# Next group's first tile turned among the last value products, mixers paced with their loads a step later, and the seventh head outputs turned beside the sixth's product

## The chip, the cores and the metric

The kernel runs on one core of a Trainium2 chip. The metric is device time in microseconds (us) from the first to the last instruction of the program with what lies around it; the median of the runs counts. TensorE (PE in the profile) does the matrix products and the transposes; VectorE (DVE), ScalarE (ACT) and GpSimd (POOL) move results out of the product banks (PSUM) and do the elementwise work; SyncE (SP) issues most of the transfers.

## The reference, cut to what matters

One step of a one-layer streaming encoder on 1024 prompt tokens and 32 sample tokens, model width 1024, everything in 32-bit floats:

```python
h = mixer(rms_norm(x, g_mix_pre))        # three parallel head groups, then cat @ w_out
x = x + rms_norm(h, g_mix_post)
h = conv_ffn(rms_norm(x, g_ffn_pre))     # up, causal conv, gelu(gate) * val, down
x = x + rms_norm(h, g_ffn_post)

# mixer
proj = xn @ w_in                          # queries, keys, values, decays and gates of all heads
o_a, s_gla  = gated_linear_scan(...)      # 6 heads, chunks of 64 tokens, masked scores + carried state
o_b, s_hg   = gated_linear_scan(...)      # 5 heads
h,  (c,n,m) = mlstm_scan(...)             # 5 heads, after a causal conv over q and k
cat = concat(head_rms_norm(o_a)*silu(.), head_rms_norm(o_b)*silu(.), head_rms_norm(h)*sigmoid(.))
return cat @ w_out
```

The states of the scans and the last rows of both convolutions are outputs too.

## The kernel before, in words

Each product of two 32-bit matrices is made of three products of rounded parts (high times high, low times high, high times low), written by one helper, `mm3`, so that lines 88, 89 and 90 of the profile are most of TensorE's work.

The program goes through the tokens in this order. **Input products:** three groups of 384, 384 and 256+32 tokens. For each group `inproj(g)` makes 14 feature products (`pf`, queries, keys, decays, with features on the partitions) and 8 blocks of value and gate products (`pv`, with tokens on the partitions; `pv1_7` is unit 1 of block 7, a unit u being 128 tokens). The group's normalised tokens are first turned by TensorE (`xt`, two banks of four 128x128 transposes a unit), then split into a high part `xh` by ScalarE and a low part `xl` by VectorE; `norm_group` is the generator that does one unit a step. **Mixers:** beside the products of the next group, `mixer(u)` runs the scans of one unit in 12 steps: the scores `sc` in steps of growing decay range (`sc0_0`, `sc0_2`, `sc0_4` for unit 0, all in one bank, each copied out by VectorE with a mask into `P` before the next may write), small transposes `mi`, the outputs `og`, `oh`, `om`, `oi` (two banks that take turns), and the normalised, gated result `cat`, which goes to memory (`cat_d`). **Output product:** for u in the order 0, 1, 2, 3, 8, 4, 5, then 6 and 7, `outproj(u)` loads `cat` again (`ct`), turns it in two halves (`ctp`), splits it (`ch`, `cl`), multiplies (`zp`, 24 products of 512 columns for each half), normalises, adds the residual, normalises again and turns the result for the FFN (`fxt`). `pipeline` interleaves the seven units of `RING`, beside the last mixers. **FFN:** up and down products by a scheme with sums of blocks ahead of and behind fewer products (`pux`, `puw`, `us`, `q`, `x` and others); at the very end four tiles `q30` to `q33` are added, squared, scaled and stored.

Generators set the rough order. `merge(main, nmain, nside)` advances the mixers' generator in step with the main one's, evenly. Within that a scheduler with a modelled timeline sets the order on each engine, moved by priorities (`high_priority`), by `issue_after` and by which bank or buffer is free: product results share three banks (`big`), scores have one (`sc`), head outputs two (`o`). Each engine goes through its own list in that order, and so do the queues that issue transfers.

Of the kernel before, what the change touches and what calls it, by code (L numbers as in the profile page):

```python
# [8 lines left out]
F32 = mybir.dt.float32  # L9
# [69 lines left out]
def body(ctx: ExitStack, tc: tile.TileContext, a: dict):  # L79
# [128 lines left out]


# [144 lines left out]
    def inproj(g, xh, xl, normed, scaled=None):  # L354
# [77 lines left out]
        def vg(blk):  # L432
            ws = vg_weights(blk)
            N = 256 if blk else 282
            for i, (u, off, n) in enumerate(units_of(g)):
# [10 lines left out]
                vg_store(blk, u, off, n, ps)  # L446
                yield
# [283 lines left out]
    def mixer(u, g, ci0):  # L731
# [17 lines left out]
        v = mx.tile([128, 704], F32, tag="v", name=f"v{u}", bufs=1)  # L749
        sp.dma_start(v[:n], v_d[t0:t0 + n, :704])  # L750
        vmt = vm[0]
        sp.dma_start(vmt[:n, :, :64], v_d[t0:t0 + n, 704:].rearrange("t (h d) -> t h d", d=64))
        gt = mx.tile([128, 1024], F32, tag="gt", name=f"gt{u}", bufs=1)
        sp.dma_start(gt[:n], g_d[t0:t0 + n, :])
# [22 lines left out]
        yield  # L777

# [24 lines left out]
        yield  # L803

# [229 lines left out]
        if u == 7:  # L1034
            ct_of[u] = cat
        else:
            sp.dma_start(cat_d[t0:t0 + n, :], cat[:n])
# [28 lines left out]
    def outproj(p2, W, u):  # L1066
# [9 lines left out]
        for hf in range(2):  # L1076
# [36 lines left out]
        def leave(ps, hf):  # L1113

            act.activation(z[:n, cs[hf]], ps[:n], AF.Square, accum_out=ss[:n, hf:hf + 1])
# [33 lines left out]
        else:  # L1149
# [11 lines left out]
        pool.tensor_tensor(ss[:n, 2:3], ss[:n, 0:1], ss[:n, 1:2], op=ALU.add)  # L1161
        rstd_of(ss[:n, 3:4], ss[:n, 2:3], n, 1, 1024)
# [27 lines left out]
        for hf in range(2):  # L1190
            p, t, b = (upper[0], "xw", 4) if u == 5 else (upper[0], *(("xw", 4), ("sx", 1))[hf]) if 5 < u < 8 else (psb, "big", 3)
# [19 lines left out]
    def pipeline(gens):  # L1211
# [5 lines left out]
        for i, x in enumerate(gens):  # L1217
            after = gens[i + 1:i + 2]
# [446 lines left out]
    def down_all(ph, pc, begun, late):  # L1665
# [43 lines left out]
        def square_of(u, n, src, half, ss):  # L1709
            jk = pc.tile([128, 512], BF16, tag="fjk", name=f"gjk{u}{half}", bufs=2)  # L1710
            act.activation(jk[:n], src, AF.Square, accum_out=ss[:n, 2 + half:3 + half])  # L1711
# [5 lines left out]
        def scale_of(n, ss):  # L1717
            pool.tensor_tensor(ss[:n, 0:1], ss[:n, 2:3], ss[:n, 3:4], op=ALU.add)  # L1718
            rstd_of(ss[:n, 1:2], ss[:n, 0:1], n, 1, 1024)
# [148 lines left out]
        for i in range(4):  # L1868
# [4 lines left out]
            dve.tensor_tensor(CA[:, i, 1], CA[:, i, 1], W[i], op=ALU.add)  # L1873
# [311 lines left out]
```

## Time and profile before

| | |
|---|---|
| runs | 1342.25, 1338.36, 1338.61 us; median 1338.61 |
| profiled execution | 1338.15 us, its span 1336.4 us |
| mean clock granted to TensorE | 0.990 |
| TensorE busy | 1295.7 us, 97% of the span |
| VectorE, ScalarE, GpSimd busy | 1009.2, 700.0, 284.6 us |

The span runs from the first to the last instruction; the 1.75 us beside it lie around it. TensorE is busy nearly always, and the view of its waits covers the rest; in some stretches its clock is granted at half (`PEclk` in the views by stretch: 1.00 is full). A wait view lists, for each line of an engine, what ended its idle time, and how often.

### The profile page before, as it was taken

To read this page: it belongs to the slowest core of one execution; us is meant where nothing else is said; L and a number is where in the kernel's file an instruction comes from. 1 tells how busy PE (TensorE), PEld (TensorE's weight loads), DVE (VectorE), ACT (ScalarE), POOL (GpSimd) and SP (SyncE) were. 2 spreads that over 40 slices of the span, in tenths; PEclk is the share of its full clock that TensorE was granted. 3 is DMA by queue.
4 is the path that set the end of the run, shared out by engine and by line. 5 is a ranking of instruction groups with operands and counts; after the bars stand their busy time and mean duration, and the time that the engine had idled before them with its cause. 6 is when DMAs were issued, how large, how long until landed. Compare 5 with 4: busy or idle time off the path is not lost.

```text
span 1336.4 us, 25589 instructions
## 1 busy us (share of the span) xinstructions
PE 1295.7 (97%) x9896; PEld 1097.9 (82%) x9896; DVE 1009.2 (76%) x1761; ACT 700.0 (52%) x1298; POOL 284.6 (21%) x400
## 2 busy tenths in 40 slices
PE   6999999998999999999999999999999999999997
PEld 6999899998898987867887777778888887778885
DVE  5795659768588778785898776778888976499556
ACT  5655556554575555444764444444555454454552
POOL 4532302135022163223110010111110000020005
PEclk9999999999998999989999999999999999999999
DMA  9799878886789954534436988864665349844425
GB/s 336 246 360 367 280 258 260 275 278 214 260 263 309 330 180 163 184 111 135 143 133 216 365 223 284 213 185 135 158 162 145 88 147 350 330 146 148 139 87 126
DMA packets 134785, 291.73 MB, mean 218 GB/s; under 512 B 29016, under 2 KB 63992, under 8 KB 132536
## 3 DMA queue, kind: packets, MB, share of 16 engines
q1 hardware_dynamic: 120887, 266.51, 58.4%
q0 software_dynamic: 9264, 19.14, 7.8%
q10 hardware_dynamic: 4512, 4.46, 1.0%
q8 instruction: 77, 1.26, 0.4%
q14 instruction: 45, 0.36, 0.1%
HBM read 229.38 MB, written 85.78 MB: 236 GB/s over the span
## 4 chain that ended last, share of the span: by engine, by line
PE 63%; DVE 9%; ACT 2%; issue 1%; POOL 1%; DMA 0%; DVEq 0%; POOLq 0%; ACTq 0%
PE pux_None L88 4%; PE pux_None L90 4%; PE pux_None L89 4%; PE puw_None L89 3%; PE puw_None L90 3%; PE puw_None L88 3%; PE q L88 3%; PE q L89 3%; PE q L90 3%; PE x L88 2%; PE x L89 2%; PE x L90 2%; PE zp L88 2%; PE zp L90 2%; PE zp L89 2%; PE us L1475 2%
## 5 line engine op out<-in xcount | busy, mean ns | idle before, releaser
L1442 DVE SCALAR_TENSOR_TENSOR y<-uu,fconv_sb,y 128x1024 f32<-128x1024 f32 x88 | 112.8, 1281 | 24.7 <-ACT y L1440 23.7
L1439 POOL COPY fhalo<-uu 128x2 f32<-128x2 f32 x44 | 19.3, 439 | 380.7 <-DVE uu L1352 380.7
L1440 ACT ACTIVATE y<-uu,fconv_sb 128x1024 f32<-128x1024 f32 x44 | 54.7, 1244 | 12.8 <-DVE uu L1352 12.2
L88 PE MATMUL pv<-wt_0h,xh 128*128 128x256 f32 (+1 forms) x192 | 56.0, 292 | 2.8 <-DVE xl L319 1.6
L90 PE MATMUL zp<-woh,cl 128*128 128x512 f32 (+1 forms) x144 | 57.0, 396 | 1.5 <-DVE cl L1091 1.5
L88 PE MATMUL zp<-woh,ch 128*128 128x512 f32 (+1 forms) x144 | 56.5, 401 | 0.7 <-ACT ch L1090 0.7
L89 PE MATMUL zp<-wol,ch 128*128 128x512 f32 (+1 forms) x144 | 56.9, 395 | 0.0
L90 PE MATMUL pv<-wt_1h,xl 128*128 128x256 f32 (+1 forms) x192 | 55.1, 287 | 0.0
L90 PE MATMUL pv<-wt_0h,xl 128*128 128x256 f32 (+1 forms) x192 | 54.8, 286 | 0.0
L88 PE MATMUL pv<-wt_1h,xh 128*128 128x256 f32 (+1 forms) x192 | 54.8, 285 | 0.0
L89 PE MATMUL pv<-wt_0l,xh 128*128 128x256 f32 (+1 forms) x192 | 54.7, 285 | 0.0
L89 PE MATMUL pv<-wt_1l,xh 128*128 128x256 f32 (+1 forms) x192 | 54.5, 284 | 0.0
L206 POOL TENSOR_SCALAR hrs<-hss 128x5 f32<-128x5 f32 (+3 forms) x27 | 10.1, 375 | 174.2 <-DVE hss L1000 170.3
L1718 POOL TENSOR_TENSOR gss<-gss 128x1 f32<-128x1 f32 (+1 forms) x9 | 9.8, 1092 | 174.2 <-ACT gjk L1711 174.2
L816 DVE COPY_PREDICATED P<-masks_sb,sc 128x352 f32<-128x352 int32 (+3 forms) x53 | 37.8, 713 | 6.0 <-PE sc L729 5.4
L88 PEld LDWEIGHTS pv<-wt_0h,xh 128*128 128x128 f32 x192 | 36.2, 188 | 4.3 <-DVE xl L319 1.9
L88 PEld LDWEIGHTS pv<-wt_1h,xh 128*128 128x128 f32 x192 | 36.2, 189 | 0.7 <-issue 0.6
L1000 DVE TENSOR_REDUCE hss<-sq 128x5 f32<-128x320 f32 (+3 forms) x27 | 13.5, 502 | 30.7 <-ACT sq L999 30.6
L207 POOL TENSOR_TENSOR hrs<-hrs,mhalf 128x5 f32<-128x5 f32 (+3 forms) x27 | 36.2, 1341 | 2.2
L90 PEld LDWEIGHTS pv<-wt_0h,xl 128*128 128x128 f32 x192 | 36.4, 189 | 0.2
L89 PEld LDWEIGHTS pv<-wt_0l,xh 128*128 128x128 f32 x192 | 36.3, 189 | 0.1
L89 PEld LDWEIGHTS pv<-wt_1l,xh 128*128 128x128 f32 x192 | 36.2, 189 | 0.1
(1899 smaller groups left out, 4639.9 us busy)
## 6 DMA issues: line engine op xcount, KB each, us to landing
wus<-in_w_us SPq DMA_DIRECT2D x16, 1024.0 KB
wrP<-in_w_dn SPq DMA_DIRECT2D x27, 512.0 KB, 3.7
ht<-h_d SPq DMA_DIRECT2D x22, 512.0 KB, 7.9
wt_0r<-in_w_tok SPq DMA_DIRECT2D x21, 512.0 KB, 6.0
wt_1r<-in_w_tok SPq DMA_DIRECT2D x21, 512.0 KB, 6.1
h_d<-y SPq DMA_DIRECT2D x21, 512.0 KB, 4.4
ws_d<-in_w_dn POOLq DMA_DIRECT2D x20, 512.0 KB, 7.0
wrP<-ws_d SPq DMA_DIRECT2D x20, 512.0 KB, 3.9
```

Source lines behind the costliest of these rows:

```text
L88: pe.matmul(ps, lh[0], rh[0], start=first, stop=False, **kw)
L89: pe.matmul(ps, lh[0], rh[1], start=False, stop=False, **kw)
L90: return pe.matmul(ps, lh[1], rh[0], start=False, stop=last, **kw)
L206: pool.tensor_scalar(out, ss, 1.0 / width, eps, op0=ALU.mult, op1=ALU.add)
L207: pool.tensor_tensor(out, out, mhalf[:n, :cols], op=ALU.pow)
L816: dve.copy_predicated(dst, mk.broadcast_to([n, 11, *mk.shape[2:]]), src)
L1000: dve.tensor_reduce(ss[:n, h0:h0 + nh], sq3, axis=mybir.AxisListType.X, op=ALU.add)
L1439: behind["POOL"] = pool.tensor_copy(fhalo[:, j, :], u[:, SEQ - 2:SEQ])
L1440: act.activation(y, u, AF.Identity, scale=fconv[:, j, 2:3], bias=fconv[:, j, 3:4])
L1442: dve.scalar_tensor_tensor(y, uu[i][:, s:s + SEQ], fconv[:, j, s:s + 1], y, op0=ALU.mult, op1=ALU.add)
L1475: kept["us"] = pe.matmul(ps[DEC * q:DEC * q + DEC], smp_x[:, k, :], ring[i % 3][:, q, :], start=k == 0, stop=k == 7)
L1718: pool.tensor_tensor(ss[:n, 0:1], ss[:n, 2:3], ss[:n, 3:4], op=ALU.add)
```

## The change

It has six parts. (1) The high and low parts of all groups lie in one pair of tiles, of which each group takes a slice, so that a transpose of the next group needs only its own columns free; and the next group's `norm_group` takes its first step right after the first unit of value block 7. (2) A mixer's loads of `v`, and of `vm` and `gt`, are issued one and two steps later, and the store of `cat` goes to GpSimd's queue in place of SyncE's. (3) In the third group the mixers are advanced by a table, `PACE`: pairs of (step of the main generator, mixer steps done by then). (4) In the output product, unit 6 yields after each half, and `pipeline` takes it as the successor of unit 5, so its halves are turned beside unit 5's product; `fxt` of unit 4 goes to the head outputs' banks. (5) The two sums of squares of a row are added by the instruction that also adds epsilon (the squares are scaled in ScalarE), which takes one GpSimd instruction from each such chain. (6) The last additions of `q` get a higher priority.

```diff
+    def rstd_of_halves(out, m0, m1, n):
+        pool.tensor_scalar(out, m0, m1, EPS, op0=ALU.add, op1=ALU.add)
+        pool.tensor_tensor(out, out, mhalf[:n, :1], op=ALU.pow)
@@ norm_tiles, inproj @@
-        return (p1.tile([128, 8, T], F32R, tag="xh", name=f"xh{g}"),
-                p1.tile([128, 8, T], F32R, tag="xl", name=f"xl{g}"))
+        if not normal:
+            normal.extend(p1.tile([128, 8, GROUPS[0][1]], F32R, name=f"x{c}_all") for c in "hl")
+        return [t[:, :, :T] for t in normal]
-    def inproj(g, xh, xl, normed, scaled=None):
+    def inproj(g, xh, xl, normed, following, scaled=None):
                 vg_store(blk, u, off, n, ps)
+                if blk == 7 and not i:
+                    next(following)
                 yield
@@ mixer: the loads of v, vm and gt leave the first step @@
-        v = mx.tile([128, 704], F32, tag="v", name=f"v{u}", bufs=1)
-        sp.dma_start(v[:n], v_d[t0:t0 + n, :704])
-        vmt = vm[0]
-        sp.dma_start(vmt[:n, :, :64], v_d[t0:t0 + n, 704:].rearrange("t (h d) -> t h d", d=64))
-        gt = mx.tile([128, 1024], F32, tag="gt", name=f"gt{u}", bufs=1)
-        sp.dma_start(gt[:n], g_d[t0:t0 + n, :])
...
         yield
+        v = mx.tile([128, 704], F32, tag="v", name=f"v{u}", bufs=1)
+        sp.dma_start(v[:n], v_d[t0:t0 + n, :704])
...
         yield
+        vmt = vm[0]
+        sp.dma_start(vmt[:n, :, :64], v_d[t0:t0 + n, 704:].rearrange("t (h d) -> t h d", d=64))
+        gt = mx.tile([128, 1024], F32, tag="gt", name=f"gt{u}", bufs=1)
+        sp.dma_start(gt[:n], g_d[t0:t0 + n, :])
...
-            sp.dma_start(cat_d[t0:t0 + n, :], cat[:n])
+            pool.dma_start(cat_d[t0:t0 + n, :], cat[:n])
@@ outproj @@
-            if u in RING:
+            if u != 7:
                 yield
-        if u not in RING:
+        if u == 7:
             yield
-            act.activation(z[:n, cs[hf]], ps[:n], AF.Square, accum_out=ss[:n, hf:hf + 1])
+            act.activation(z[:n, cs[hf]], ps[:n], AF.Square, scale=1.0 / 32, accum_out=ss[:n, hf:hf + 1])
-        pool.tensor_tensor(ss[:n, 2:3], ss[:n, 0:1], ss[:n, 1:2], op=ALU.add)
-        rstd_of(ss[:n, 3:4], ss[:n, 2:3], n, 1, 1024)
+        rstd_of_halves(ss[:n, 3:4], ss[:n, 0:1], ss[:n, 1:2], n)
-            p, t, b = (upper[0], "xw", 4) if u == 5 else ...
+            p, t, b = (psm, "o", 2) if u == 4 else (upper[0], "xw", 4) if u == 5 else ...
-    def pipeline(gens):
+    def pipeline(gens, then):
-            after = gens[i + 1:i + 2]
+            after = (gens + [then])[i + 1:i + 2]
@@ end of the FFN @@
-            pool.tensor_tensor(ss[:n, 0:1], ss[:n, 2:3], ss[:n, 3:4], op=ALU.add)
-            rstd_of(ss[:n, 1:2], ss[:n, 0:1], n, 1, 1024)
+            rstd_of_halves(ss[:n, 1:2], ss[:n, 2:3], ss[:n, 3:4], n)
-            dve.tensor_tensor(CA[:, i, 1], CA[:, i, 1], W[i], op=ALU.add)
+            with tc.high_priority(offset=AHEAD):
+                dve.tensor_tensor(CA[:, i, 1], CA[:, i, 1], W[i], op=ALU.add)
@@ merge and the calls @@
-    def merge(main, nmain, nside):
+    def merge(main, nmain, nside, pace=None):
             want = (i + 1) * nside // nmain
+            for (i0, s0), (i1, s1) in zip(pace or (), (pace or ())[1:]):
+                if i0 <= i < i1:
+                    want = s0 + (i + 1 - i0) * (s1 - s0) // (i1 - i0)
+    PACE = ((0, 0), (3, 3), (10, 12), (17, 15), (NIN, 3 * NMIX))
+    normed = [norm_group(g, *norm_tiles(g)) for g in range(3)] + [None]
-        merge(inproj(g, *xs_, norm_group(g, *xs_), scaled), NIN, n_side)
+        merge(inproj(g, *xs_, *normed[g:g + 2], scaled), NIN, n_side, PACE if g == 2 else None)
-    merge(pipeline(firsts), 26, 3 * NMIX + 2)
+    last = [outproj(p2, wo, u) for u in (6, 7)]
+    merge(pipeline(firsts, last[0]), 26, 3 * NMIX + 2)
     pump(1000)
-    last = [outproj(p2, wo, u) for u in (6, 7)]
-    for x in (last[0], last[0], last[1]):
+    for x in last:
         next(x)
```

What the edits do to the order, at three places. First TensorE at the end of group 0, where unit 0's scores and the last value products meet (`pv1_7`, `pv2_7`: units 1 and 2 of block 7; `xt30`: the first half of unit 3's tokens). Before (the rows begin at `pv1_7`'s last three of 24 products):

```order
L88 MATMUL pv1_7_1638<-wt0_7_1h_1602,xh0_162 128x256
L89 MATMUL pv1_7_1638<-wt0_7_1l_1603,xh0_162 128x256
L90 MATMUL pv1_7_1638<-wt0_7_1h_1602,xl0_163 128x256
L729 MATMUL mi_159<-ident_123,kh0_1891 128x128
L729 MATMUL sc0_2_2090<-Qz1_153,k0_1816 64x2x32
L729 MATMUL sc0_2_2090<-Qz1_153,k0_1816 64x32
L729 MATMUL sc0_2_2090<-Qz1_153,k0_1816 64x2x32
L729 MATMUL sc0_2_2090<-Qz1_153,k0_1816 64x32
L729 MATMUL sc0_2_2090<-Qz1_153,k0_1816 64x2x32 x4
L729 MATMUL sc0_2_2090<-Qz1_153,k0_1816 64x32 x2
L88 MATMUL pv2_7_1669<-wt0_7_0h_1595,xh0_162 128x256
```

and now, from the last of `sc0_0` on:

```order
L738 MATMUL sc0_0_1978<-Qz0_152,Ld0_150 32x32 x8
L738 MATMUL mi_159<-ident_123,kh0_1886 128x128
L322 MATMUL xt30_1638<-ident_123,x3_1144 128x128 x4
L738 MATMUL mi_159<-ident_123,kh0_1886 128x128 x3
L738 MATMUL sc0_2_2088<-Qz1_153,k0_1828 64x2x32
L738 MATMUL sc0_2_2088<-Qz1_153,k0_1828 64x32
L738 MATMUL sc0_2_2088<-Qz1_153,k0_1828 64x2x32
L738 MATMUL sc0_2_2088<-Qz1_153,k0_1828 64x32
L738 MATMUL sc0_2_2088<-Qz1_153,k0_1828 64x2x32 x4
L738 MATMUL sc0_2_2088<-Qz1_153,k0_1828 64x32 x4
L322 MATMUL xt31_1645<-ident_123,x3_1144 128x128 x4
...
L88 MATMUL pv1_7_1652<-wt0_7_0h_1595,xh_all_162 128x256
```

`pv1_7` stood between `sc0_0` and `sc0_2` and now stands behind both, with unit 3's transposes in its place.

Next TensorE in the seventh unit's mixer, behind its second group of scores. Before:

```order
L88 MATMUL zp81_8323<-woh7_6898,ch81_8034 32x512
L89 MATMUL zp81_8323<-wol7_6906,ch81_8034 32x512
L90 MATMUL zp81_8323<-woh7_6898,cl81_8035 32x512
L1086 MATMUL ctp41_8386<-ident_123,ct4_7889 128x128 x4
L1195 MATMUL fxt30_8395<-ident_123,z3_7845 128x128 x4
L729 MATMUL sc7_4_8179<-Qz1_153,Ld1_151 64x2x32
L729 MATMUL sc7_4_8179<-Qz1_153,Ld1_151 64x32
```

and now:

```order
L738 MATMUL sm7_8105<-ident_123,mqk7_7899 128x64
L1205 MATMUL fxt30_8387<-ident_123,z3_7838 128x128 x4
L1205 MATMUL fxt31_8393<-ident_123,z3_7838 128x128 x4
L88 MATMUL zp40_8429<-woh0_6887,ch40_8246 128x512
...
L90 MATMUL zp40_8429<-woh7_6894,cl41_8384 128x512
L1097 MATMUL ctp50_8458<-ident_123,ct5_8239 128x128 x4
L738 MATMUL sc7_4_8171<-Qz1_153,Ld1_151 64x2x32
L738 MATMUL sc7_4_8171<-Qz1_153,Ld1_151 64x32
```

The third group of scores, `sc7_4`, followed four transposes; now the 24 products of `zp40` (its first and last stand here) and another tile's transposes lie ahead of it.

Last TensorE between unit 5's output product (`zp51` is its second half) and unit 6's. Before:

```order
L90 MATMUL zp51_8566<-woh7_6898,cl51_8509 128x512
L1195 MATMUL fxt40_8593<-ident_123,z4_8437 128x128 x4
L1195 MATMUL fxt41_8599<-ident_123,z4_8437 128x128 x4
L1086 MATMUL ctp60_8616<-ident_123,ct6_8465 128x128 x4
L1086 MATMUL ctp61_8625<-ident_123,ct6_8465 128x128 x4
L88 MATMUL zp60_8635<-woh0_6891,ch60_8621 128x512
L89 MATMUL zp60_8635<-wol0_6899,ch60_8621 128x512
```

and now:

```order
L90 MATMUL zp50_8529<-woh7_6894,cl51_8500 128x512
L1097 MATMUL ctp60_8556<-ident_123,ct6_8456 128x128 x4
L88 MATMUL zp51_8565<-woh0_6887,ch50_8463 128x512
...
L90 MATMUL zp51_8565<-woh7_6894,cl51_8500 128x512
L1205 MATMUL fxt40_8601<-ident_123,z4_8428 128x128 x4
L1097 MATMUL ctp61_8592<-ident_123,ct6_8456 128x128 x4
L1205 MATMUL fxt41_8607<-ident_123,z4_8428 128x128 x4
L88 MATMUL zp60_8624<-woh0_6887,ch60_8561 128x512
L89 MATMUL zp60_8624<-wol0_6895,ch60_8561 128x512
```

Unit 6's first half (`ctp60`) was turned behind all of `zp51` and is turned ahead of it; the second (`ctp61`) stands between the two `fxt40`, `fxt41`.

More of the change, by code (lines that the diff above doesn't have):

```diff
@@ L272, in norm_tiles @@
         T = GROUPS[g][1] + GROUPS[g][2]
-        return (p1.tile([128, 8, T], F32R, tag="xh", name=f"xh{g}"),
-                p1.tile([128, 8, T], F32R, tag="xl", name=f"xl{g}"))
+        if not normal:
+            normal.extend(p1.tile([128, 8, GROUPS[0][1]], F32R, name=f"x{c}_all") for c in "hl")
+        return [t[:, :, :T] for t in normal]
+    normal = []
     xn_of, vgi, vcopies, gate = {}, [], [], []
@@ L1156, in outproj @@
                 with tc.high_priority(offset=AHEAD):
-                    kept["jk"] = act.activation(jk, pss[hf], AF.Square, accum_out=ss[:, hf:hf + 1])
+                    kept["jk"] = act.activation(jk, pss[hf], AF.Square, scale=1.0 / 32, accum_out=ss[:, hf:hf + 1])
         load_res(u)
@@ L1190, in outproj @@
         for hf in range(2):
-            p, t, b = (upper[0], "xw", 4) if u == 5 else (upper[0], *(("xw", 4), ("sx", 1))[hf]) if 5 < u < 8 else (psb, "big", 3)
+            p, t, b = (psm, "o", 2) if u == 4 else (upper[0], "xw", 4) if u == 5 else (upper[0], *(("xw", 4), ("sx", 1))[hf]) if 5 < u < 8 else (psb, "big", 3)
             ps = p.tile([128, 4, 128], F32, tag=t, name=f"fxt{u}{hf}", bufs=b)
@@ L1710, in square_of @@
             jk = pc.tile([128, 512], BF16, tag="fjk", name=f"gjk{u}{half}", bufs=2)
-            act.activation(jk[:n], src, AF.Square, accum_out=ss[:n, 2 + half:3 + half])
+            act.activation(jk[:n], src, AF.Square, scale=1.0 / 32, accum_out=ss[:n, 2 + half:3 + half])
         def norm_of(u, n, src, half, ss):
```

## Prediction

> **What bounds the kernel.** I read the page first, for the engines' shares and the clock; then TensorE's waits, which say what its idle time is made of; then the timeline around each long one; and last the views by stretch, for the granted clock.
>
> ```profile
> span 1336.4 us, 25589 instructions
> PE 1295.7 (97%) x9896; PEld 1097.9 (82%) x9896; DVE 1009.2 (76%) x1761; ACT 700.0 (52%) x1298; POOL 284.6 (21%) x400
> ...
> PE xt L315 <- DVE x L295: 9.6, 1, 9.6
> PE sc L729 <- DVE P L816: 3.4, 3, 2.4
> PE ctp L1086 <- DMA ct<-cat_d: 1.5, 1, 1.5
> ```
>
> TensorE is the bound: its 1295.7 us leave 40.7 us of the span, of which 9.6 are the start (first wait row) and, by the tail's rows below, 9.6 the end (the last product is done at 1326.76). So 21.5 us of idle time lie between, in many places of at most 2.4, and no other engine is near its limit over the whole. The change can only remove or add such places, and shorten the end. The clock is the second thing to win. It was granted at half in four places ahead of the end; three follow a long wait:
>
> ```profile
> 326.25:329.66 3.41, 1.72 (x67) 1.40 (x68) 3.41 (x9) 3.39 (x8) 1.35 (x2) 1.00 0.72 166
> 329.66:333.07 3.41, 3.41 (x16) 3.40 (x16) 3.41 (x14) 1.70 (x5) 1.93 (x2) 0.50 0.67 268
> 411.60:415.00 3.40, 1.82 (x71) 1.81 (x71) 3.39 (x8) 1.69 (x4) 0.39 (x2) 1.00 1.05 366
> 415.00:421.80 6.80, 6.80 (x62) 6.19 (x62) 5.91 (x13) 1.43 (x4) 0.00 (x0) 0.50 0.75 210
> 493.50:496.90 3.40, 3.24 (x54) 2.56 (x52) 3.21 (x11) 3.40 (x4) 3.03 (x5) 1.00 0.78 192
> 496.90:500.30 3.40, 3.40 (x28) 3.01 (x26) 3.34 (x5) 3.40 (x5) 0.00 (x0) 0.50 1.01 319
> 585.70:589.10 3.40, 0.96 (x20) 0.75 (x22) 3.39 (x9) 1.51 (x4) 1.33 (x4) 1.00 0.67 200
> 589.10:595.90 6.80, 6.80 (x119) 6.13 (x111) 6.36 (x12) 1.15 (x2) 0.44 (x2) 0.50 0.23 76
> ```
>
> The columns behind the stretch are its length, then TensorE's busy time, weight loads, VectorE, ScalarE, GpSimd, and the clock. A stretch of 3.4 us in which TensorE was busy for 1.72, 1.82 or 0.96 us is followed by 3.4 or 6.8 us at 0.50. Ahead of the fourth (493.5) it was busy for 3.24. In 3.4 us at half clock TensorE does at most 1.7 us of work, so each costs at most 1.7, less where what runs in it hangs on other engines. [...]
>
> **The change, place by place.** A gain has a plus.
>
> *Groups 0 to 1: unit 3's transposes ahead of `sc0_2`, `pv1_7` behind it.*
>
> ```profile
> 141.72 0.39 PE L88 MATMUL pv<-wt_0h,xh 128*128 128x256 f32 x1 [0.83 <-DVE vth L425]
> 144.60 0.52 DVE L816 COPY_PREDICATED P<-masks_sb,sc 128x352 f32<-128x352 int32 x1
> 145.22 0.54 PE L729 MATMUL sc<-Qz,k 64*64 64x64 f32 x20 [0.28 <-PE mi L729]
> 145.40 0.68 DVE L836 TENSOR_TENSOR x<-b 128x512 f32<-128x512 f32 x1
> ```
>
> `pv1_7` fills 141.72 to about 144.8, and meanwhile VectorE gets to the masked copy of `sc0_0` (done at 145.12), for which `sc0_2` must wait since scores have one bank. VectorE's order up to that copy is the same afterwards. So `xt30` starts at 141.72 in place of `pv1_7` (the same bank comes free), takes about 0.7 us, the `mi` 0.4, and from about 142.9 TensorE stands until 145.2: 2.3 us that `pv1_7` covered. Then `pv1_7` waits for the split of `xt30`, whose VectorE half comes behind the row at 145.40 and takes 0.68: 146.76, another 0.4 us. The transposes themselves are only moved (1.3 us less later), and a gap of 0.3 us behind them goes. Bounds: 0, if VectorE were free sooner, and -2.9; I take -2.4. The cover is gone here, so the clock counts: of any 3.4 us from 142 on, TensorE would be busy for about 1.0, within the three rows above. One stretch at half clock, of which 2 us hold large products, costs 1.0 to 1.7: I take -1.2. Sum -3.6.
>
> *Groups 1 to 2.*
>
> ```profile
> 322.44 0.81 PE L729 MATMUL oi<-C,mqz 128*64 128x65 f32 x20 [0.90 <-DVE cat L1002]
> 325.43 0.66 PE L315 MATMUL xt<-ident,x 128*128 128x128 f32 x4 [0.72 <-ACT vth L98]
> 329.45 0.45 PE L88 MATMUL pv<-wt_0h,xh 128*128 128x282 f32 x1 [1.64 <-DVE xl L319]
> ```
>
> Unit 6's transposes now stand behind `pv3_7`, covered; but `oi2`, now ahead of `pv5_7`, meets VectorE's `cat` some 0.8 us too early in addition to its 0.90, and `pv5_7` waits about 0.55 for `xl`. Against that the 0.72 goes and the 1.64 shrinks, since one unit's turn is left to do there. The half-clock stretch behind 329.66 may move to 323 or go. Bounds -1.5 and +3; I take +0.8.
>
> *Group 2, paced.*
>
> ```profile
> 368.20 0.75 PE L729 MATMUL oh<-S,qz 128*64 128x64 f32 x20
> 384.28 0.80 PE L729 MATMUL oi<-C,mqz 128*64 128x65 f32 x20 [0.84 <-DVE cat L1002]
> 398.82 0.44 PE L729 MATMUL mi<-ident,kh 128*128 128x128 f32 x2 [0.38 <-ACT kt L877]
> 401.66 0.55 PE L729 MATMUL sc<-Qz,k 64*64 64x64 f32 x24 [0.68 <-DVE P L816]
> 413.18 1.14 PE L729 MATMUL sc<-Qz,Ld 64*64 64x64 f32 x64 [2.15 <-DVE e L543]
> ```
>
> `oi3` needs the bank of `oh3`, and with it VectorE's `cat` of `oh3`, which came only some 15 us behind `oh3` (368.95 to 384.28), since the group's gate rows stand ahead of it on VectorE. `oi3` moves from 95 feature products behind `oh3` to 53, but those gate rows now lie behind `cat`: laid end to end from the durations of before, `cat` is done about 8 us behind `oh3` and `oi3` reached after about 9. So +0.84; if the gate rows come in between after all, 42 products of cover are missing, 5 us by the value products' 0.12 each (24 from 141.72 to about 144.8), and it is -3. `sc4_0` and `sc4_2` find their operands ready (+0.38, +0.68). `sc4_4` still has 48 feature products for cover, about 8.1 us with the small ones; but VectorE no longer has the mLSTM score product (0.68), a decay product (0.42) and some of the convolution (0.5 each) between `sc4_2` and its second masked copy, so that chain, laid end to end, is about 8.7 us, where it was about 10.3: a wait of 0.6 remains of 2.15 (+1.5). With that wait shorter the stretch at 411.6 is fuller; two at half clock cost up to 3.4, and I count half of a loss of 3.0, since the fourth dip shows that small products can bring one too (+1.5). Sum +4.9, bounds 0 and +6.8.
>
> *Mixer 7.* The wait, and two rows for the price of an output product:
>
> ```profile
> 588.87 1.43 PE L729 MATMUL sc<-Qz,Ld 64*64 64x64 f32 x49 [2.44 <-DVE P L816]
> 623.89 0.39 PE L90 MATMUL zp<-woh,cl 128*128 128x512 f32 x1
> 625.25 0.39 PE L90 MATMUL zp<-woh,cl 128*128 128x512 f32 x1
> ```
>
> From 623.89 to 625.25 there are six products, 0.227 us each. So the 24 of `zp40` are 5.4 us of work between the same two points, over twice the 2.44: the wait goes (+2.4). `zp40`'s operands hang on `ctp41`, which stands ahead too. The stretch 585.7 to 589.1 would be full, and the two at half clock go: they lose up to 3.4 us, part of it small products that are not clock-bound; I take +2.4. Behind `sc7_4`, `og7` now has 13 products (3.0 us) for its chain where it had 24, and `oi7` comes about 5.0 us behind `oh7` where `cat`'s chain took about 4.3: bound 0 to -1.0, I take -0.3. Sum +4.5.
>
> *From unit 5 to unit 6.*
>
> ```profile
> 626.93 1.26 PE L1086 MATMUL ctp<-ident,ct 128*128 128x128 f32 x8 [0.42 <-DVE z L1199]
> 628.93 0.50 PE L88 MATMUL zp<-woh,ch 128*128 128x512 f32 x1 [0.75 <-ACT ch L1090]
> 631.12 0.50 PE L90 MATMUL zp<-woh,cl 128*128 128x512 f32 x1 [1.46 <-DVE cl L1091]
> ```
>
> With `ctp60` 24 products earlier, its split is done 5 us before `zp60`, whose first 14 products need only that half; those 3.2 us cover the second half's. `fxt40` no longer needs a bank of the three. So 0.42+0.75+1.46 = 2.63 go, less some 0.2: +2.4, bounds +1 and +2.6.
>
> *Loads, stores, the GpSimd addition.* No load of `v`, `vm` or `gt` stands among TensorE's waits, so there is slack of a size that I don't know: 0, bounds 0 and -2. SyncE's queue is held less by them. The stores of `cat` go behind GpSimd, 21% busy, which made `cat` itself. One addition less in a chain of TensorE's own only counts in unit 7's: +0.3, bounds 0 and +0.7.
>
> *The end.*
>
> ```profile
> 1326.37 0.39 PE L90 MATMUL q<-P3w,P3h 128*128 128x512 f32 x1
> 1326.11 1.42 DVE L1732 SCALAR_TENSOR_TENSOR fr<-ca,gss,fr 128x512 f32<-128x512 f32 x2 [0.72 <-POOL gss L207]
> 1328.71 0.68 DVE L1873 TENSOR_TENSOR ca<-ca,q 128x512 f32<-128x512 f32 x1
> 1330.28 0.70 POOL L1718 TENSOR_TENSOR gss<-gss 128x1 f32<-128x1 f32 x1 [2.35 <-ACT gjk L1711]
> 1331.93 1.41 DVE L1732 SCALAR_TENSOR_TENSOR fr<-ca,gss,fr 128x512 f32<-128x512 f32 x2 [0.99 <-POOL gss L207]
> ```
>
> The last addition (1328.71) is moved ahead of two scalings of the tile before it: about 1327.8. GpSimd's addition (0.70) goes, but then the next instruction is the first behind the wait and may take as long, so 0.2 to 0.7 us are won. The last scalings start at about 1330.5: +1.4, bounds +0.9 and +2.0.
>
> *What the new order brings that I cannot see.* Hundreds of rows change places, and TensorE's small waits come back elsewhere in other sizes; three of the size of the 0.75 ahead of `zp60`: -2.0, bounds 0 and -6.
>
> The sum: -3.6 +0.8 +4.9 +4.5 +2.4 +0.3 +1.4 -2.0 = +8.7 against the profiled 1338.15, so 1329.45. The median of the runs is 0.46 above that execution, so **1329.9** is forecast.
>
> **The rivals.** *The clock does not follow the waits.* Ahead of the fourth dip TensorE was busy for 3.24 of 3.40 us, so something else can set it: the mix of small score products, which no edit takes away. Then the dips of group 2 and mixer 7 stay or come again a little later, and none is added at groups 0 to 1: the three clock terms (-1.2, +1.5, +2.4) go, the gain is 6.0, and the time 1332.6. Against it speak the three stretches of 0.96 to 1.82 us. [...]
>
> *The waits move.* The removed stalls are chains on VectorE, 76% busy and nearly full in those stretches (3.39 of 3.40 us in two of the rows above). What TensorE no longer waits for it may wait for at the next bank: of the wait terms of group 2 and mixer 7 (3.4+2.4) half come back, groups 1 to 2 lose 1.5 in place of 0.8 won, and the unseen term reaches -4. The gain is 8.7-2.9-2.3-2.0 = 1.5, 1337.1: no change by the bound of 0.3% (4.0 us), which is about what a measurement of this kernel can tell. For it speaks that groups 0 to 1 show such a new wait already; against it, that mixer 7 gets 5.4 us of true cover.
>
> *Slower: the stores on GpSimd's queue.* A load of `ct` may start only when `cat` is in memory, and stands in SyncE's queue with the weights and residuals behind it.
>
> ```profile
> g_d<-vg POOLq DMA_DIRECT2D x32, 128.0 KB, 4.8
> cat_d<-cat SPq DMA_DIRECT2D x7, 512.0 KB, 2.9
> L1037 SPq DMA_DIRECT2D cat_d<-cat x8: 317/320/583, 228.0 to 586.1; - x8
> L255 SPq DMA_DIRECT2D ct<-cat_d x8: 372/409/639, 462.1 to 599.8; - x8
> ```
>
> GpSimd's stores take 4.8 us to land where SyncE's of `cat` took 2.9. If each of seven units' transposes waited 1.9 us more, that is 13.3: 8.7-13.3 = -4.6, 1343.2. It decides where a load is asked for less than 4.8 us behind its store. Against it: the first store is at 228 and the first load at 462; the last is stored at 586 and loaded at 599.8. Only unit 1's load was late (the 1.5 row), for another reason, as it stood behind a load of gates.
>
> **Chances.** The forecast as summed, 0.47; the clock rival, 0.24; the moved waits, 0.21; the stores, 0.05; and 0.03 for other losses of that size, of the loads a step later above all (-2 at each of several mixers). The first two are faster, the third the same, the last two slower; of the first two some 0.03 falls short of 4 us. So faster 0.68, same 0.24, slower 0.08. The range reaches from 1323.5 (the upper bounds of group 2, mixer 7's clock and the end, and no unseen waits) to 1338, which takes in nearly all of the moved waits; the forecast's own is 1325 to 1333.
>
> **What would show it.** In the profile after: `sc0_2` with over 1.5 us idle before it near 143 and a clock under 1.00 behind; no `P` wait over 1 us and a clock of 1.00 in mixer 7; no row for `cl` or `ch` before `zp60`; a wait of `sc4_4` under 1 us; the last scalings less than 4 us behind the last product. I am wrong if TensorE's idle time between start and end is not below 17 us, or if the waits on `ct` grow.

## The result and the profile after

The changed kernel takes 1328.07 us (median of four runs, 1327.38 to 1328.59), where the kernel before took 1339.73 us in the runs beside it (1338.36 to 1342.25): a ratio of 0.991, 95% interval 0.989 to 0.993. A second measurement gave 1327.11 us (six runs, 1324.55 to 1330.46), ratio 0.990 (0.988 to 0.992). Forecast were 1329.9 us, 1323.5 to 1338. The page, and TensorE's waits:

```profile
span 1326.7 us, 25586 instructions
PE 1291.3 (97%) x9896; PEld 1094.9 (83%) x9896; DVE 1008.1 (76%) x1761; ACT 699.3 (53%) x1298; POOL 287.2 (22%) x390
...
PE xt L322 <- DVE x L302: 9.5, 1, 9.5
PE mi L738 <- ACT kt L888: 5.2, 2, 3.1
PE pv L88 <- ACT vf L486: 1.5, 3, 1.2
PE ctp L1097 <- DVE cl L1102: 1.5, 1, 1.5
PE puy_None L90 <- DVE A_1h L94: 1.2, 1, 1.2
PE oi L738 <- DVE cat L1013: 1.2, 1, 1.2
PE ctp L1097 <- DMA ct<-cat_d: 0.7, 1, 0.7
```

Of the 9.7 us that the span is shorter, 5.3 are idle time of TensorE and 4.4 busy time of the same 9896 products. Both traces have six windows of 3.4 us at half clock (0.50) ahead of the end. By an estimate (the time from one product's start to the next, against the median of the same product at full clock) these windows cost 10.5 us before and 9.6 after, so they explain about 1 us of the 4.4; where the rest lies is open. Between the start and the end TensorE is idle for 16.7 us, where it was for 21.4. The waits of the scores for `P` fell from 3.4 us to 0.6, those for `e` and `ch` are gone, and those for `xl` and `cl` fell from 1.6 and 2.9 to 1.0 and 1.5; the wait for `kt` (two times, 5.2 us) grew from 0.4. Where the 9.7 us were won and lost is read by laying the same product of both traces side by side (the 24th product of each `pv`, `pf` or `zp` and so on) and following the difference of their times along the program. The readings come from one execution of each kernel; the second trace of the changed kernel loses up to 2.5 us against the first between 500 and 520 us, in the same order, so smaller differences at one place say little:

| stretch (us of before) | difference at its end | won here | forecast |
|---|---|---|---|
| start, group 0 (to 139) | +0.2 | +0.2 | 0 |
| groups 0 to 1 (to 192) | -3.3 | -3.5 | -3.6 |
| groups 1 to 2 (to 370) | +1.3 | +4.5 | +0.8 |
| group 2 (to 488) | +2.9 | +1.6 | +4.9 |
| output product up to mixer 7 (to 560) | +2.2 | -0.7 | (unseen) |
| mixer 7 (to 611) | +7.4 | +5.2 | +4.5 |
| unit 5 to 6 (to 642) | +10.9 | +3.5 | +2.4 |
| start of the FFN (to 700) | +9.2 | -1.7 | +0.3 |
| the end | +9.7 | +0.5 | +1.4 |

At 370 us of before, among group 2's feature products, both kernels have run the same TensorE instructions, kind by kind, so the two rows that meet there can be told apart.

Three of the places, as stretches of the same length near the same point of the program, first before, then after (length, then busy time of TensorE, its weight loads, VectorE, ScalarE, GpSimd; then the clock):

```profile
140.00:150.00 10.00, 8.89 (x138) 8.15 (x131) 8.06 (x24) 6.87 (x17) 5.03 (x7) 1.00 0.63 205
560.00:605.00 45.00, 42.36 (x540) 31.31 (x540) 35.55 (x85) 17.39 (x44) 11.98 (x18) 0.92 0.48 157
618.00:633.00 15.00, 12.38 (x60) 9.66 (x59) 7.84 (x13) 7.17 (x15) 3.82 (x8) 1.00 0.42 128
```

```profile
140.00:150.00 10.00, 7.08 (x89) 5.73 (x85) 8.70 (x25) 6.38 (x17) 4.37 (x6) 0.68 0.60 200
555.00:600.00 45.00, 44.79 (x586) 32.98 (x582) 38.14 (x88) 19.17 (x48) 14.10 (x18) 1.00 0.45 141
611.00:626.00 15.00, 15.00 (x75) 12.55 (x75) 8.71 (x14) 7.96 (x17) 4.27 (x7) 1.00 0.42 140
```

The first place is the loss: 49 of TensorE's products and transposes fewer in the same 10 us, and a clock of 0.68. The other two are full, at full clock.

### The profile page after: what moved, and what is told of

Read it like the earlier page. It is cut to its first block, busy times and chain, and to the rows that moved or that the text cites. A ratio compares the mean times of both kernels' runs of the same rounds, so it can differ in the third digit from the quotient of the medians.

```text
span 1326.7 us, 25586 instructions
## 1 busy us (share of the span) xinstructions
PE 1291.3 (97%) x9896; PEld 1094.9 (83%) x9896; DVE 1008.1 (76%) x1761; ACT 699.3 (53%) x1298; POOL 287.2 (22%) x390
## 4 chain that ended last, share of the span: by engine, by line
PE 74%; DVE 14%; DMA 4%; ACT 4%; issue 2%; POOL 1%; SPq 0%; DVEq 0%; ACTq 0%; POOLq 0%
PE pux_None L88 4%; PE pux_None L90 4%; PE pux_None L89 4%; PE pv L88 3%; PE puw_None L90 3%; PE puw_None L88 3%; PE puw_None L89 3%; PE q L88 3%; PE q L90 3%; PE q L89 3%; PE pv L90 3%; PE pv L89 3%; PE x L88 2%; PE x L90 2%; PE x L89 2%
## 5 line engine op out<-in xcount | busy, mean ns | idle before, releaser
L88 PE MATMUL pv<-wt_0h,xh_all 128*128 128x256 f32 (+1 forms) x192 | 56.4, 293 | 1.2 <-DVE xl_all L326 1.0
L90 PE MATMUL pv<-wt_0h,xl_all 128*128 128x256 f32 (+1 forms) x192 | 54.9, 286 | 0.0
L89 PE MATMUL pv<-wt_0l,xh_all 128*128 128x256 f32 (+1 forms) x192 | 54.7, 285 | 0.0
L88 PE MATMUL pv<-wt_1h,xh_all 128*128 128x256 f32 (+1 forms) x192 | 54.4, 283 | 0.0
L89 PE MATMUL pv<-wt_1l,xh_all 128*128 128x256 f32 (+1 forms) x192 | 54.3, 283 | 0.0
L90 PE MATMUL pv<-wt_1h,xl_all 128*128 128x256 f32 (+1 forms) x192 | 54.2, 283 | 0.0
L88 PEld LDWEIGHTS pv<-wt_0h,xh_all 128*128 128x128 f32 x192 | 36.5, 190 | 2.7 <-DVE xl_all L326 1.6
L89 PEld LDWEIGHTS pv<-wt_0l,xh_all 128*128 128x128 f32 x192 | 36.6, 190 | 0.1
L90 PEld LDWEIGHTS pv<-wt_0h,xl_all 128*128 128x128 f32 x192 | 36.5, 190 | 0.1
L88 PEld LDWEIGHTS pv<-wt_1h,xh_all 128*128 128x128 f32 x192 | 36.1, 188 | 0.3 <-issue 0.2
```

What stands on the lines that cost most here:

```text
L88: pe.matmul(ps, lh[0], rh[0], start=first, stop=False, **kw)
L89: pe.matmul(ps, lh[0], rh[1], start=False, stop=False, **kw)
L90: return pe.matmul(ps, lh[1], rh[0], start=False, stop=last, **kw)
```

## The experiments

My theory was that gains and losses stand at their places and add up; the rivals are named with each run. Each kernel was run in five rounds beside the kernel before; ratios are to that one, with 95% intervals. For comparison: the changed kernel has 1328.07 us and 0.991.

**No early turn in group 0** (for group 2 it stays):

```diff
-                if blk == 7 and not i:
+                if blk == 7 and not i and g:
                     next(following)
```

> The changed kernel (1328.1 us), but the next group's first tile is not turned among group 0's last value products; among group 1's it still is. Theory (stall of 2 us ahead of the small transposes and the scores, and half clock behind it, cost 3.5 us net there): the time falls to about 1324.7 us, no TensorE wait over 1 us and a clock of 1.00 between 140 and 150 us, and from group 1 on everything is as in the changed kernel. Rival (waits move: what is won at 143 us is waited for later in group 1): 1327.5 to 1328.5 us.

Measured: 1335.52 us, ratio 0.996 (0.994 to 0.998), 7.5 us more than the changed kernel. In the trace the stall at 143 us and its half clock are gone, as expected, and by 192 us it is 1.9 us ahead of the changed kernel; it would be more, but a window at half clock begins at 174.45, behind one in which TensorE was busy throughout. By 485 us that is down to 0.3, as `oi2` now waits 1.95 where it waited 1.18, with half clock behind it; and then 7.5 us are lost between 485 and 618 us, some 350 us behind the edit:

```profile
141.59 0.39 PE L88 MATMUL pv<-wt_0h,xh_all 128*128 128x256 f32 x1 [0.31 <-DVE vth L432]
145.09 0.54 PE L738 MATMUL sc<-Qz,k 64*64 64x64 f32 x20 [0.28 <-PE mi L738]
...
508.62 0.73 PE L738 MATMUL om<-vm,w 32*32 32x65 f32 x10 [1.09 <-DVE cat L1013]
511.92 0.87 PE L738 MATMUL oi<-C,mqz 128*32 128x65 f32 x10 [1.99 <-issue]
550.27 0.92 PE L738 MATMUL og<-v,P 64*64 64x64 f32 x24 [1.18 <-DVE P L827]
573.25 0.41 PE L88 MATMUL zp<-woh,ch 128*32 128x512 f32 x1 [1.58 <-DVE z L1209]
```

The reason stands in the program, not in the hardware: the scheduler's modelled times moved, and it wrote another order there. `sc7_4` now stands in the middle of `zp81`, and `og7` behind 16 products of it. So neither my theory nor the rival holds: the wait did not move along in time, the order changed.

**No early turn at all:**

```diff
-                if blk == 7 and not i:
-                    next(following)
```

> The changed kernel without any early turn, in group 0 or group 1; the shared tiles, pacing and all else stay. Theory: the first is worth -3.4 us and the second a gain of some 1.5 us (the waits of 0.7 and 1.6 us and half clock around 325 to 333 us), so about 1326.2 us, and a wait for xl over 1 us near 328 us with half clock behind it comes back. Rival (the second turn is what won most of the 6 us between 300 and 480 us, the pacing little): about 1329 to 1330 us.

Measured: 1328.82 us, 0.992 (0.990 to 0.994), like the changed kernel. TensorE's order from the output product on is word for word the same, and the difference can be read place by place (a plus where this kernel is ahead): +4.0 us by 192, -5.6 between 295 and 407, +1.7 between 485 and 520 in the same order, and +1.4 at the FFN's start. So in this trace the turn in group 0 costs 4.0 us, and the one in group 1 is worth 5.6, which I had at 0.8; but up to 1.7 of the 5.6 are a window at half clock at 353.03, behind one in which TensorE was busy throughout. The time is the rival's: the second turn won most of the 6 us between 300 and 480, the pacing little. Both turns together win nothing that the runs can tell. What the second takes away:

```profile
321.62 0.80 PE L736 MATMUL oi<-C,mqz 128*64 128x65 f32 x20 [0.96 <-DVE cat L1011]
324.61 0.66 PE L322 MATMUL xt<-ident,x 128*128 128x128 f32 x4 [0.71 <-ACT vth L98]
328.64 0.40 PE L88 MATMUL pv<-wt_0h,xh_all 128*128 128x282 f32 x1 [1.64 <-DVE xl_all L326]
...
325.72:329.13 3.41, 1.77 (x69) 1.45 (x62) 3.41 (x8) 3.41 (x8) 1.35 (x2) 1.00 0.82 180
329.13:332.54 3.41, 3.41 (x18) 3.40 (x16) 3.41 (x14) 1.42 (x4) 1.65 (x1) 0.50 0.60 240
```

In the changed kernel the same place has waits of 1.18 and 0.51 and no half clock.

**Mixers not paced:**

```diff
-        merge(inproj(...), NIN, n_side, PACE if g == 2 else None)
+        merge(inproj(...), NIN, n_side, None)
```

> The changed kernel with the mixers advanced evenly in the third group. Prediction's term (pacing is worth 4.9 us): 1333 us, with a wait of sc4_4 near 2 us and half clock for 6.8 us around 415 us. Rival (the paced order has a new wait of 3.1 us for kt and 3.4 us of half clock of its own, so that it wins about 1.5 us): 1329.6 us.

Measured: 1337.94 us, 0.999 (0.997 to 1.000). Up to 485 us it is 4.6 us behind the changed kernel. That is near the forecast's 4.9, but the forecast was against the kernel before, and the chain on VectorE, which is back at its place, is longer than there (4.04 us where that had 2.15), with three windows at half clock behind it in place of two:

```profile
411.58 0.70 PE L738 MATMUL sc<-Qz,Ld 64*64 64x64 f32 x16 [4.04 <-DVE e L552]
...
509.27 1.08 PE L1097 MATMUL ctp<-ident,ct 128*128 128x128 f32 x4 [3.36 <-DMA ct<-cat_d]
```

The other 5.2 us up to 620 us are again lost in an order of the output product in which the seventh mixer's scores cut up `zp80` and `zp81`; a wait for `ct` of 3.36 us is among them.

**Unit 6 not turned beside unit 5's product:**

```diff
-            after = (gens + [then])[i + 1:i + 2]
+            after = gens[i + 1:i + 2]
...
-            if u != 7:
+            if u in RING:
                 yield
-        if u == 7:
+        if u not in RING:
             yield
...
-    for x in last:
+    for x in (last[0], last[0], last[1]):
```

> The changed kernel, but unit 6's halves are turned behind unit 5's product as before, in one step (fxt of unit 4 stays in the head outputs' banks). Theory: only the stretch from unit 5 to unit 6 changes, the waits for ch and cl ahead of zp60 come back, 2 to 2.6 us, and perhaps half clock behind them: 1330.1 to 1331.5 us. Rival (the banks for fxt alone took the waits away): 1328.1 us. Second rival (mixer 7's order hangs on it too): wait of 2.4 us and half clock near 585 us come back, 1335 us.

Measured: 1331.26 us, 0.993 (0.991 to 0.995), 3.2 us more than the changed kernel. In TensorE's order only that stretch and some rows at the FFN's start differ; both waits are back, with half clock behind them:

```profile
621.29 0.50 PE L88 MATMUL zp<-woh,ch 128*128 128x512 f32 x1 [1.03 <-ACT ch L1101]
623.40 0.50 PE L90 MATMUL zp<-woh,cl 128*128 128x512 f32 x1 [1.38 <-DVE cl L1102]
...
620.82:624.23 3.41, 1.56 (x6) 0.99 (x7) 3.41 (x6) 1.92 (x4) 0.00 (x0) 1.00 0.53 154
624.23:627.64 3.41, 3.41 (x10) 2.63 (x9) 3.38 (x6) 1.74 (x3) 0.61 (x1) 0.50 0.71 193
```

5.0 us are lost here, and 1.4 come back at the FFN's start. Both rivals are out: the banks for `fxt` alone do not take the waits away, and mixer 7 stays as it is in the changed kernel.

**Turn only for group 2, one step earlier.** This kernel computes unit 3's last value block from unit 6's tokens; the instructions are the same in number and size.

```diff
-                if blk == 7 and not i:
+                if (blk == 6 and i == 2) if g else 0:
                     next(following)
```

> The changed kernel, but unit 3's tokens are turned where they were before (no early turn in group 0), and unit 6's one step earlier still, behind group 1's value block 6. The order of TensorE in the output product is the changed kernel's. Theory (losses and gains stay at their places as long as the order behind them is the same): +3.7 us at 143 us, no half clock there; at 315 to 330 us the two held banks cost up to 2 us; so 1324.5 to 1326.5 us. Rival (what is won early is waited for later): 1328 us.

Measured: 1324.22 us, 0.989 (0.986 to 0.991). The order behind is the changed kernel's, and against that kernel 2.9 us are won at group 0, 1.7 lost at groups 1 to 2, 1.2 won up to the FFN and 1.4 at its start. So the gain and the loss that the edit made did stay at their places, as the order behind them did. The other 2.6 us were won where the order is the same, so a place's price moves by 1 to 1.5 us without an edit, and the time came out 0.3 us below the forecast.

**The sums of squares added apart again:**

```diff
     def rstd_of_halves(out, m0, m1, n):
-        pool.tensor_scalar(out, m0, m1, EPS, op0=ALU.add, op1=ALU.add)
-        pool.tensor_tensor(out, out, mhalf[:n, :1], op=ALU.pow)
+        pool.tensor_tensor(out, m0, m1, op=ALU.add)
+        rstd_of(out, out, n, 1, 1)
```

> The changed kernel, with the two sums of squares added by a GpSimd instruction of their own again (all else as changed). With this TensorE's order in the seventh mixer is the one of before: sc7_4 four transposes behind sm7. Theory (mixer 7's gain is the order's, and the order hangs on the length of the GpSimd chain that the scheduler reckons with): a wait near 2.4 us ahead of sc7_4 and half clock for up to 6.8 us near 580 us come back, 1332 to 1334 us, most of it between 560 and 610 us. Rival (the instruction itself is what counts, in unit 7's chain and at the end): 1328.1 to 1329 us.

Measured: 1332.55 us, 0.995 (0.993 to 0.997), 4.5 us more than the changed kernel. Up to 485 us the two traces are within 0.4 us; at 577 this one is 0.4 us ahead and at 608 4.9 behind, with the wait and the half clock of before:

```profile
586.43 1.22 PE L738 MATMUL sc<-Qz,Ld 64*64 64x64 f32 x64 [2.79 <-DVE P L827]
```

Its order in mixer 7 is that of before. So the gain of mixer 7 hangs on an instruction of 0.2 to 0.7 us on GpSimd: without it the scheduler's times shift, and `zp40` comes ahead of `sc7_4`. It does not hang on it alone: the kernel without group 0's turn and the one without pacing lack that instruction too, and lost the order all the same.

**The kernel before, with that part alone** (the squares scaled as in the change):

```diff
-        pool.tensor_tensor(ss[:n, 2:3], ss[:n, 0:1], ss[:n, 1:2], op=ALU.add)
-        rstd_of(ss[:n, 3:4], ss[:n, 2:3], n, 1, 1024)
+        rstd_of_halves(ss[:n, 3:4], ss[:n, 0:1], ss[:n, 1:2], n)
...
-            pool.tensor_tensor(ss[:n, 0:1], ss[:n, 2:3], ss[:n, 3:4], op=ALU.add)
-            rstd_of(ss[:n, 1:2], ss[:n, 0:1], n, 1, 1024)
+            rstd_of_halves(ss[:n, 1:2], ss[:n, 2:3], ss[:n, 3:4], n)
```

> The kernel before with one part of the change alone, the sums of squares added by the instruction that adds epsilon. TensorE's order is that of before up to the sixth mixer; from there zp80 and zp81 are cut up by the seventh mixer's scores, as in the two kernels that lost 6 to 7.5 us there. Theory (the order decides): 1340 to 1343 us, no gain, the tail within 0.6 us of before. Rival (one GpSimd instruction less per chain is a gain by itself): 1338 us or less.

Measured: 1339.63 us, 0.999 (0.997 to 1.001): no gain. The order from the sixth mixer on is the one that cuts up `zp80` and `zp81`. Only the end is 0.5 us shorter (9.08 us behind TensorE's last product, in place of 9.62). In the kernel before the edit does not shorten mixer 7 (its trace is 0.7 us longer there); in the changed kernel the gain does not come without it.

**Stores of `cat` on SyncE's queue:**

```diff
-            pool.dma_start(cat_d[t0:t0 + n, :], cat[:n])
+            sp.dma_start(cat_d[t0:t0 + n, :], cat[:n])
```

> The changed kernel with the stores of cat on SyncE's queue again; TensorE's and VectorE's orders are word for word those of the changed kernel. My term for it is 0: 1328.1 us, within 1 us, and the waits on ct near 504 us within 0.5 us of 0.65. Rival (a store on GpSimd's queue lands later, or SyncE's queue is held less by it): over 1 us of difference between 500 and 520 us, either way.

Measured: 1326.26 us, 0.990 (0.987 to 0.993). Against the changed kernel the trace has no wait for `ct` (there 0.65) and 0.97 for `cl` (there 1.48), and wins 1.5 us between 485 and 618 us. But the kernel without turns, which leaves the stores alone, wins 1.7 at the same place, and the second trace of the changed kernel waits 1.37 and 1.68 there. The forecast missed by 0.8 us beyond its bound, and the rival's sign is there (1.3 us between 500 and 520). Still, with the two traces of one kernel further apart than that, my 0 is not refuted, and a price of about a microsecond is not excluded.

**No turn in group 0, and the stores on SyncE's queue:**

```diff
-                if blk == 7 and not i:
+                if blk == 7 and not i and g:
...
-            pool.dma_start(cat_d[t0:t0 + n, :], cat[:n])
+            sp.dma_start(cat_d[t0:t0 + n, :], cat[:n])
```

> The changed kernel with two parts undone: no early turn in group 0, and the stores of cat on SyncE's queue. Each alone left (first) an order that cut up zp80 and zp81 in the seventh mixer, 1335.5 us, and (second) 1326.3 us. Together the order has all of zp40 between sc7_2 and sc7_4 again. Theory (the order in the seventh mixer decides, the stall of group 0 is gone): no wait of 2 us at 143 us, no wait over 1.2 us between 560 and 600 us, 1322.5 to 1325.5 us, faster than both kernels. Rival (the loss of 7 us without the first early turn is the turn's own): 1333 us or more.

Measured: 1331.49 us, 0.992 (0.990 to 0.995). In mixer 7 no wait over 1.2 us is left, as expected, but in the order that comes with it the sample tokens' mixer (unit 8) lets `om` and `oi` wait 1.17 and 2.03 near 512 us, with half clock behind them. It is not faster than the changed kernel.

**The same, with unit 3 turned behind the last unit of block 7:**

```diff
-                if blk == 7 and not i and g:
+                if blk == 7 and i == (2 if not g else 0):
```

> As the run before, but unit 3's tokens are turned behind the last unit of group 0's value block 7 and not with the next group's first step; in the seventh mixer the same order as there. Theory: the turn there costs and wins nothing, since sc0_2 already stands behind pv1_7: within 1 us of the run before. Rival (transposes that wait for a bank ahead of the scores): a wait over 1 us between 145 and 157 us, 1 to 2 us more than the run before.

Measured: 1330.67 us, 0.992 (0.991 to 0.994), within 1 us of the run before it, as the theory had it; but the six runs of that one spread over 10 us (1326.23 to 1336.15), so this shows little. The forecast of 1322.5 to 1325.5 for the pair failed by 5 to 6 us. Against the changed kernel's trace the place near 510 us costs 4.3 us in the first and 0.9 in the second, and both lose about 2.8 us between 595 and 620, where `om` waits 1.19 us and half clock follows.

**The changed kernel again:**

> The changed kernel itself, beside the two runs before it on the same chip: 1327.4 to 1328.7 us, if the difference between runs of one kernel on two chips is small against 2 us.

Measured: 1327.11 us, 0.990 (0.988 to 0.992). That is 0.3 us below the forecast. Its six runs spread over 6 us, and its profiled run is 1.6 us behind the first one in the same order. No kernel here that computes all of the reference beats the changed one by more than its runs differ. The loads a step later, the shared tiles alone and the other banks for `fxt` of unit 4 were not undone alone, so their worth is open.

## Why the prediction was right

The total was right within 2 us, in part by luck: the terms of groups 1 to 2 and of group 2 missed by 3.7 and 3.3 us in opposite directions. The other places came out within about 1 us, except the FFN's start (-1.7 in place of +0.3), but not all for the reason that I gave.

*Groups 0 to 1* (-3.6, measured -3.5): right, except that the waiting instruction was the second `mi`, not `sc0_2`. It waits for ScalarE's copy of `kt`; the scores behind it could not have come before the masked copy's end at 144.93 either:

```profile
141.53 0.66 PE L322 MATMUL xt<-ident,x 128*128 128x128 f32 x4 [0.86 <-DVE vth L432]
142.02 0.27 PE L738 MATMUL mi<-ident,kh 128*128 128x128 f32 x1
144.35 0.69 PE L738 MATMUL mi<-ident,kh 128*128 128x128 f32 x2 [2.06 <-ACT kt L888]
144.40 0.53 DVE L827 COPY_PREDICATED P<-masks_sb,sc 128x352 f32<-128x352 int32 x1
145.04 0.87 PE L738 MATMUL sc<-Qz,k 64*64 64x64 f32 x24
```

The half clock behind it came (0.50 from 143.55 to 150.38 us), and for two windows, not one, while the idle time grew by only 1.5 us (1.4 to 2.9) where I summed 2.4: a smaller wait and a larger clock term make up the sum. In the kernels without the turn 1.5 to 4.0 us come back.

*Groups 1 to 2* (+0.8, measured 4.5): mis-sized. I let the half clock "move or go" and counted nothing for it; with 1.2+0.5 us of idle in place of 3.3 it goes (the clock is 1.00 from 324.46 to 331.28 us), which by estimate, half of 3.41 us, is worth up to 1.7. All idle time there fell by 1.3 us; the rest of the 4.5 is not explained.

*Group 2* (+4.9, measured 1.6): mis-sized. The waits that I named went, 4.1 us in all. But the paced order has a price that I did not see, a new wait for `kt` of 3.1 us near 392 with half clock behind it (0.50 from 396.14 to 399.55 us), and some small waits grew, so that TensorE's idle time there hardly fell (5.3 to 5.0 us) where I had 3.4; the gain is about the one window at half clock that is left out of two. The 4.6 us of the run without pacing are against another kernel than the one before. That the two terms together give 6.1 against 5.7 is luck.

*Mixer 7* (+4.5, measured 5.2) and *unit 5 to 6* (+2.4, measured 3.5): the waits went as told; the second was mis-sized by about 1 us, which is busy time at full clock and not explained. The small products that I took as not bound by the clock were slowed too: 49 of the scores took 1.43 us at half clock (the prediction's row at 588.87), and 64 of them take 1.14 at full clock in the changed kernel. What the prediction lacks is the cause of mixer 7's gain. I read the gain off the new order and did not ask which part makes that order. It needs the part that I priced at 0.3 us in a chain, through the scheduler, together with others, and not the successor of unit 5: without that the order there stays.

*The unseen term* (-2.0): -0.7 in the output product, and -1.7 at the FFN's start, in place of +0.3. There `puy` waits 1.22 us where before the longest wait was 0.67, and half clock follows. In the output product TensorE's idle time fell by 0.8 us, but a second window at half clock came (0.50 from 491.71 to 498.54 us, where before it was from 496.92 to 500.33).

*The end* (+1.4, measured 0.5): GpSimd's addition went, and its neighbour took longer instead. Of the two chains, before (from the prediction's row at 1330.28 to the scalings at 1331.93) 1.65 us, now 1.86:

```profile
1320.33 1.18 POOL L211 TENSOR_SCALAR gss<-gss 128x1 f32<-128x1 f32 x1 [1.09 <-ACT gjk L1721]
1321.60 0.56 POOL L212 TENSOR_TENSOR gss<-gss,mhalf 128x1 f32<-128x1 f32 x1
1322.19 1.42 DVE L1741 SCALAR_TENSOR_TENSOR fr<-ca,gss,fr 128x512 f32<-128x512 f32 x2 [0.84 <-POOL gss L212]
```

What was won there is the earlier last addition: it starts 1.16 us behind TensorE's last product, where it started 1.95 behind. The higher priority for it changes nothing: without it every engine's order is the same, word for word. What moved it is again the joined addition, through the order. The first row is of the changed kernel with the sums added apart, the second of the kernel before with that part alone:

```profile
1323.09 0.68 DVE L1883 TENSOR_TENSOR ca<-ca,q 128x512 f32<-128x512 f32 x1
1329.43 0.68 DVE L1876 TENSOR_TENSOR ca<-ca,q 128x512 f32<-128x512 f32 x1
```

They stand 1.96 and 1.17 us behind their last products (1321.13 and 1328.26), and the stretch behind the last product is 9.62 us in the kernel before and in the first, 9.08 in the changed kernel and in the second. One sign did not come: the last scalings start 4.6 us behind the last product, not less than 4.

*The range.* The bounds that I name for its lower end add up to 5.5 us, which is 1324.4 and not 1323.5.

*The clock rival* is out as stated: two windows at half clock were added at groups 0 to 1, and those of mixer 7 went. In the traces of before, of the changed kernel and of the eleven runs above I cut TensorE's time into windows of 3.41 us whose edges the changes of the clock give (in the changed kernel half clock begins at 143.55, 396.14, 491.71 and 662.38 us and lasts 6.83, 3.41, 6.83 and 3.41), and listed the windows at full clock in which it was busy for less than three quarters. Of the 34 that were busy for at most 0.53, 33 were followed by half clock; of the 57 from 0.57 to 0.75, seven. But its ground stays in part: of the 58 stretches at half clock ahead of the end, 16 came behind a window that was busy for 0.95 or more, twelve of them near 490 us, the prediction's fourth dip, and four between 171 and 350. In these some nine in ten of TensorE's products have 65 columns or fewer, but so it is in 179 other full windows that half clock did not follow. The kernel before with the joined addition has one at 175 us, where TensorE's order is that of the kernel before, which has none:

```profile
171.59:175.00 3.41, 3.41 (x42) 2.39 (x40) 2.74 (x5) 3.19 (x6) 0.18 (x1) 1.00 1.02 398
175.00:178.40 3.40, 3.40 (x20) 3.11 (x17) 2.68 (x6) 1.74 (x4) 0.00 (x0) 0.50 0.71 292
```

It comes out of that place 1.5 us later. No run here says what sets the clock there. For the stalls, the same waits in two traces show that their place in the window mattered there:

```profile
658.96:662.37 3.41, 1.74 (x5) 0.87 (x6) 3.41 (x7) 2.44 (x6) 0.00 (x0) 1.00 0.00 0
662.37:665.78 3.41, 3.41 (x9) 2.67 (x9) 3.41 (x6) 0.00 (x0) 0.00 (x0) 0.50 0.00 0
```

```profile
660.23:663.64 3.41, 2.19 (x9) 1.48 (x9) 3.41 (x6) 1.06 (x3) 0.00 (x0) 1.00 0.00 0
663.64:667.05 3.41, 3.41 (x19) 2.84 (x18) 3.38 (x5) 1.22 (x2) 0.00 (x0) 1.00 0.00 0
```

The changed kernel is the first pair, the one without turns the second. Both have waits of 0.31 and 1.22 us here; in the first they fall so that 1.74 of 3.41 us are busy, in the second 2.19, and only the first pays, by 1.4 us: half clock came there behind waits of 1.22 us and less. *The moved waits* came true in group 2 (the new 3.1 us for `kt`, and idle time all but unchanged) and not in mixer 7; *the stores* showed no more than 1.5 us.

## What to carry to other kernels

Where a scheduler with a modelled timeline writes the order, an edit's largest effect can stand hundreds of microseconds behind it, in an order that no one wrote; before pricing a part by its own instructions, compare the order of the busy engine with and without that part alone. Edits of this kind are not additive: undo each alone on the changed kernel, and say against which kernel a worth is told (pacing: 4.6 us against the changed kernel without it, 1.6 against the kernel before). Look at what a short stall leaves of the time around it, too: here the same wait of 1.22 us was followed by half clock (0.50) where TensorE was busy for 1.74 of a window's 3.41 us, and not where it was for 2.19, a difference of 1.4 us.

## What the hardware showed that I had not expected

Two rows group GpSimd's instructions by line (least, median and longest duration in ns): of the changed kernel, which adds a per-row operand and a constant, and of the kernel before, which takes two constants.

```profile
L211 POOL TENSOR_SCALAR oss<-oss x9: 298/302/1338, 511.2 to 644.2; 128x1 f32<-128x1 f32 x8, 32x1 f32<-32x1 f32 x1
```

```profile
L206 POOL TENSOR_SCALAR oss<-oss x18: 180/191/1898, 514.4 to 661.7; 128x1 f32<-128x1 f32 x16, 32x1 f32<-32x1 f32 x2
```

The first took 0.30 us where the second took 0.19; at the end of the program 1.18 where the addition and the form with constants took 0.70 and 0.19. Taking an instruction out of such a chain by joining two made the chain no shorter there (1.86 us, before 1.65); what the end won came through VectorE's order.

In the thirteen traces half clock came behind 33 of the 34 windows in which TensorE was busy for 0.53 or less, whether `sc` waited for `P` (2.44 us, before), `mi` for `kt` (3.10, after) or `puy` for `A_1h` (1.22, after), and behind seven of 57 from 0.57 to 0.75; it came behind 16 that were busy for 0.95 or more as well. The windows lie elsewhere in the program from trace to trace: in the changed kernel's two, half clock begins at 143.55 and at 145.07 us. That the same program therefore pays for a given stall in one run and not in another is my guess, and that this makes the 6 us between runs of the changed kernel is not shown (a window at half clock cost 1.6 to 1.75 us by the estimate from products' starts, and the two traces have six and seven of them).
